# Reading the two parts of x in turns: 4, 16 or 64 columns at a time in a TensorE product

## The chip, the cores and the metric

The kernel runs on one core of one Trainium2 chip. The metric is device time in microseconds (us) of one execution, the median of several. The core's engines run side by side: TensorE (PE, with its weight loads as PEld), VectorE (DVE), ScalarE (ACT), GpSimd (POOL) and the queue that issues transfers (SP).

## What is computed

Two layers over 256 tokens of width 1024, all in float32. Layer 0 mixes tokens with a chunked gMLP, layer 1 with attention over 16 heads; after each mixer comes a gated MLP of width 2816 with a causal convolution of width 3. Each of the four sub-layers is `x <- LayerNorm(alpha * x + f(x))`. The lines of the reference that the change touches:

```python
def chunked_gmlp(x, w_in, ln_g, ln_b, w_s, b_s, w_out):
    z = jax.nn.gelu(x @ w_in)
    u, v = jnp.split(z, 2, axis=-1)
    ...
    return (u * sv.reshape(B, S, GMLP_WIDTH)) @ w_out

def moba_attention(x, w_qkv, w_o, rel_bias):
    qkv = (x @ w_qkv).reshape(B, S, 3, H, Dh)
    ...

def conv_ffn(x, w_up, conv_w, conv_b, w_down):
    h = x @ w_up
    ...
    return (jax.nn.gelu(g) * val) @ w_down
```

The products `x @ w_in` (its u half), `x @ w_qkv` (its query and key parts) and `x @ w_up` of layer 0 are the ones in question.

## The kernel before

**Two parts of each factor.** TensorE multiplies in float32r, a rounded form of float32. To keep float32 accuracy, each factor is split by `split` into a rounded part and the rest: weights into `whi` and `wlo`, activations into the high and low part that both lie in the tile `xt`. A product is then three products: high by high, high by low, and low by high.

**Where x lies.** `xt` holds, for each of the 8 blocks `k` of 128 input features, 512 columns: 256 tokens of the high part, and right behind them the same 256 tokens of the low part. `both[:, k]` is that run of 512 columns.

**Products by columns.** `cols_apart` (line 714) computes an output block of 128 features by 256 tokens. The weights stand in the array and x is streamed past them. In its first pass, for each of 8 `k`, one matmul with the weights `whi` streams all 512 columns of `both[:, k]`, and writes 512 columns of one accumulation bank: `whi` by x's high part into the first 256, `whi` by x's low part into the second 256. In its second pass, 8 matmuls with the weights `wlo` stream the 256 high columns alone and add to the second half. ACT then copies the second half out and DVE adds the first to it. `cols_apart` serves u in `gmlp` (stage `a_u`, 8 output blocks), queries and keys in `project` of `moba` (stage `b_qk`, 16 blocks), and 20 of the 22 block pairs of each up-projection in `conv_up` (stages `f_up0` and `f_up1`, 40 blocks each). The output bank is a tile called `bank`, or half of a tile called `twos`; in the up-projections the two kinds alternate.

**Order of the work.** All groups of instructions are recorded with an estimated cost and put in an order by `Plan.emit`; the cost of a matmul is taken from the number of its columns. `mms` (line 332) records a group, and line 344 in it issues every matmul of the stages in question. Each matmul comes with a weight load of its own, which the profile lists as PEld.

Of the kernel before, what the change touches and what calls it, by code (L numbers as in the profile page):

```python
# [35 lines left out]
HALF = 512  # L36
# [14 lines left out]
SOON = 5000.0  # L51
LEAD = 1700.0
WARM = 9


class Buf:
# [187 lines left out]
def trunk_kernel(ctx: ExitStack, tc: tile.TileContext, a: dict, out: bass.AP):  # L244
# [15 lines left out]
    both = xt.rearrange("p (k x) -> p k x", k=KT)  # L260
# [44 lines left out]
    def bank(long=False):  # L305
        free = [i for i in ALONE if not bank_of[i][2]]
        return taken(min(free, key=lambda i: bank_of[i][0]), long) if free else half(long)
# [18 lines left out]
    def done_with(b):  # L326
        for i in range(BANKS):
            if bank_of[i][1] is b:
                bank_of[i] = (bank_of[i][0], b, False)


    def mms(seq, r, w, fill=False, into=None, ready=False, share=1, turn=0.0):

        ns = 0.0
        for o, l, x, _, _ in seq:
            n = flat(x)
            ns += max(107.0, n / 2.4) + 2.5 if l.dtype == F32R else (218.0 if n <= P else n / 0.6 + 5)

        def emit():
            if into is not None and not ready:  # L340
                return

            for o, l, x, start, stop in seq if into is None else [q for _, _, q in sorted(into, key=lambda q: q[:2])]:
                nc.tensor.matmul(o, l, x, start=start, stop=stop)  # L344
        return plan.op("pe", ns / share + turn, emit, r, w, fill)
# [136 lines left out]
    def sub(name, c, s):  # L482
        return chunks[where[name, c]][s]

    def spent(name, c):
        i = where[name, c] + CHUNKS
        if i < len(stream):
            prep(i)
# [10 lines left out]
    def xt_new():  # L499
        return xth.new(), xtl.new()  # L500
# [4 lines left out]
    xh, xl = xt_new()  # L505
# [205 lines left out]
        plan.tick()  # L711
        return groups

    def cols_apart(*tiles):


        ops = []
        for low in (False, True):
            for b, at, h, l, hi, lo in tiles:
                o, wt = b.ap[:, at:at + HALF], lo if low else hi  # L720
                for k in range(KT):
                    ks, parts = slice(k * P, (k + 1) * P), [(t, k) for t in range(NT)]
                    seq = [(o[:, S:], wt.ap[:, ks], both[:, k, :S], False, k == KT - 1)] if low else \
                        [(o, wt.ap[:, ks], both[:, k], k == 0, False)]
                    ops.append(mms(seq, [(wt, [k // 2]), (h, parts)] + [(l, parts)] * (not low), [(b, [at])]))
                    plan.tick()
        return ops
# [76 lines left out]
    def xt_at(h, l):  # L804
        return lambda k, t: (xt_view(h)[:, t, k, :], xt_view(l)[:, t, k, :], [(h, [(t, k)]), (l, [(t, k)])])


    def gmlp():
        at = xt_at(xh, xl)
        pieces = [[(o, HALF, bank(True)) for o in (0, HALF)] for _ in range(NT)]  # L810
        order = [(k, t) for k in range(4) for t in range(NT)] + [(k, t) for t in range(NT) for k in range(4, KT)]
        v = []
        into, steps = [[] for _ in range(4)], {}
        for k, t in order:
            steps[k, t] = rows_step(pieces[t], *at(k, t), *sub("a_v", k // 2, k % 2), k == 0, k == KT - 1,
                                    into[k] if k < 4 else None)
            if (k, t) == (5, NT - 1):

                for j in (6, 7):
                    for o in steps[j, 0]:  # L820
                        o.after = steps[k, t][-1]
            if t == NT - 1 and k % 2:
                spent("a_v", k // 2)
            if (k, t) == (3, NT - 1):
                rows = ln_rows(0)
                ws, bs = load_mixer()
            if k == KT - 1:
                vt = place("ff", HALF + t * D, D)
                for o, n, b in pieces[t]:
                    act(vt.ap[:, o:o + n], b.ap, AF.Gelu_apprx_tanh, [b], [(vt, range(o // S, (o + n) // S))],  # L830
                        psum=True, table="gelu")
                    done_with(b)
                st, mean, rstd = stats(vt, vt.ap, [(0, HALF), (HALF, HALF)])
                scaled(vt, vt.ap, st, mean, rstd, rows)
                v.append(vt)
        load_rest()
        mh, ml = place("rr", 0, KT * S), place("rr", KT * S, KT * S)
        hv, lv = (b.ap.rearrange("p (k s) -> p k s", k=KT) for b in (mh, ml))
        uring = Places("ff", [0, S, HALF + 2 * D, HALF + 2 * D + S], S)
        yring = Places("ff", range(5120, 6144, S), S)  # L840
        uparts = Ring(tiles("uparts", 2, S))
        us = {}

        def spatial(gs):
            bs4 = [half() for _ in gs]
            o = mms([(b.ap[:, c * P:(c + 1) * P], v[c].ap[:, g * P:(g + 1) * P], ws[1][:, g, :], True, True)
                     for b, g in zip(bs4, gs) for c in range(NT)],
                    [(v[c], sorted({g // 2 for g in gs})) for c in range(NT)] + [ws[0]], bs4, fill=True)
            for b, g in zip(bs4, gs):
                y = yring.new()  # L850
                y3 = y.ap.rearrange("p (c t) -> p c t", c=NT)
                tt(y3, b.ap[:, :S].rearrange("p (c t) -> p c t", c=NT), bs[1][:, g:g + 1, :].to_broadcast([P, NT, P]),
                   ALU.add, [b, bs[0]], [y])
                if g < GROUPS // 2:
                    tt(y.ap, y.ap, us[g].ap, ALU.mult, [y, us[g]], [y])
                else:
                    plan.op("pool", 1060, lambda y=y, g=g: nc.gpsimd.tensor_tensor(y.ap, y.ap, us[g].ap, op=ALU.mult),
                            [y, us[g]], [y])
                split((mh, [g], hv[:, g, :]), (ml, [g], lv[:, g, :]), (y, [0], y.ap))
            return o  # L860

        for c in range(GROUPS // 2):
            pair = [bank(), bank()]
            ops = cols_apart(*((b, 0, xh, xl, *sub("a_u", c, j)) for j, b in enumerate(pair)))
            if c == 2:
                visit.after = ops[2 * KT - 1]
            spent("a_u", c)
            for g, b in zip((2 * c, 2 * c + 1), pair):
                us[g], part = uring.new(), uparts.new()
                for o in (act(part.ap, b.ap[:, S:], AF.Copy, [b], [part], psum=True),  # L870
                          tt(us[g].ap, b.ap[:, :S], part.ap, ALU.add, [b, part], [us[g]])):
                    o.early = SOON
                act(us[g].ap, us[g].ap, AF.Gelu_apprx_tanh, [us[g]], [us[g]], table="gelu")
            if c % 2:
                visit = spatial(range(2 * c - 2, 2 * c + 2))
        visit.after = ops[2 * KT - 1]
        return lambda k, t: (hv[:, k, t * P:(t + 1) * P], lv[:, k, t * P:(t + 1) * P], [(mh, [k]), (ml, [k])])


    def conv_up(layer, h, l):  # L880
# [6 lines left out]
        name = f"f_up{layer}"  # L887
# [45 lines left out]
        for t in range(NT):  # L933
            b = half()
# [13 lines left out]
        for n, i in enumerate(range(2, FT, 2)):  # L948
            subs = [sub(name, i + x, j) for x in range(2) for j in range(2)]
            if n % 2:  # L950
                bs = [two_banks(x) for x in range(2)]
                cols_apart(*((bs[m // 2], m % 2 * HALF, h, l, *s) for m, s in enumerate(subs)))
            else:
                bs = [bank() for _ in subs]
                cols_apart(*((b, 0, h, l, *s) for b, s in zip(bs, subs)))
            for x in range(2):
                spent(name, i + x)
                gate(i + x, joined(bs[x]) if n % 2 else joined_apart(bs[2 * x:2 * x + 2]), psum=False)
# [3 lines left out]
    def moba(h, l, scr):  # L962
# [28 lines left out]

        def project(i, visit=None):
            bs = [bank(), bank()]
            ops = cols_apart(*((bs[j], 0, h, l, *sub("b_qk", i, j)) for j in range(2)))
            if visit:
                visit(ops[2 * KT - 1])
            for j in range(2):
                part(i, j, bs[j])
            return ops[-1]
# [116 lines left out]
        n = PAIRS - 1  # L1116
# [20 lines left out]
    h, l = project_out("a_out", KT, at, xtok, 0, 1)  # L1137
    at = conv_up(0, h, l)
    scr = build_bias(10 * S)
    h, l = project_out("f_dn0", FT, at, xtok, 1, 2)  # L1140
    at = moba(h, l, scr)
    h, l = project_out("b_o", KT, at, xtok, 2, 3)
# [7 lines left out]
    ones = nc.const_aps.tensor(1.0, (P, HALF), mybir.dt.bfloat16)  # L1150
    for _ in range(WARM):
        nc.tensor.matmul(banks[-1], ones[:, :P], ones, start=True, stop=True)
# [82 lines left out]
```

## Time and profile before

| | |
|---|---|
| median of 3 runs | 561.52 us (561.39 to 561.65) |
| span of the profiled execution, first to last instruction | 560.6 us |
| PE busy | 553.1 us, 99% of the span, 3042 matmuls |
| PEld busy | 474.3 us, 85% |
| DVE busy | 470.9 us, 84% |
| ACT busy | 369.9 us, 66% |
| POOL busy | 15.0 us, 3% |
| HBM read | 109.36 MB, 197 GB/s over the span |

The profiled execution's span is 0.9 us under the median of the timed runs; that part lies around the first and last instruction. Matmuls overlap in the pipeline, so that the mean of one (391 ns for 512 columns) is the time from its start to its end, not the distance to the next. The rate of TensorE is read from starts: the difference between the starts of two pieces, divided by the matmuls of the first.

### The profile page before, as it was taken

The numbers are of one execution on the slowest core, as the hardware profiler recorded it, in microseconds if no ns is written. First come the engines' busy times: TensorE is split into PE (matmuls) and PEld (weight loads), VectorE is DVE, ScalarE is ACT, GpSimd is POOL, SyncE is SP. The second block draws the span as 40 slices with busy tenths as digits, with TensorE's granted clock in tenths as the row PEclk, the third lists the DMA queues.
The fourth block names the chain that finished last, engine by engine and source line by source line (L and its number), as shares of the span: only waits on it lengthen the run. The fifth ranks groups of instructions, "written<-read, shape, count | busy, mean of one in ns | idle before, by whom it ended". The sixth has DMA issues, their size and how long they took to land.

```text
span 560.6 us, 8337 instructions
## 1 busy us (share of the span) xinstructions
PE 553.1 (99%) x3042; PEld 474.3 (85%) x3042; DVE 470.9 (84%) x918; ACT 369.9 (66%) x700; POOL 15.0 (3%) x22
## 2 busy tenths in 40 slices
PE   9999999999999999999999999999999999999995
PEld 6889888988888888888888888788888988888884
DVE  5799989999998989467957788888999999998627
ACT  6657577786777767245567867578777787696601
POOL 0021110000000000001000000000000000000001
PEclk9999999999999999999999999999999999999999
DMA  8989414766555265752666351825757555467202
GB/s 321 374 317 329 175 75 161 290 233 229 214 188 189 80 248 214 260 220 76 229 221 198 104 189 76 300 77 176 275 205 275 196 188 189 166 215 292 79 0 77
DMA packets 19569, 110.98 MB, mean 198 GB/s; under 512 B 2294, under 2 KB 5576, under 8 KB 7368
## 3 DMA queue, kind: packets, MB, share of 16 engines
q1 hardware_dynamic: 19240, 110.18, 54.7%
q8 instruction: 24, 0.39, 0.3%
q10 hardware_dynamic: 288, 0.26, 0.1%
q14 instruction: 17, 0.14, 0.1%
HBM read 109.36 MB, written 1.07 MB: 197 GB/s over the span
## 4 chain that ended last, share of the span: by engine, by line
PE 96%; DVE 2%; DMA 1%; issue 0%; DVEq 0%; ACT 0%; ACTq 0%
PE bank L344 62%; PE twos L344 32%; PE twos L350 1%; PE bank L350 1%; DMA ff<-in_head 1%; DVE x L366 1%; DVE ff L366 0%; DVE stat L592 0%; DVE stat L632 0%; DVE whi L387 0%; DVE ff L635 0%; DVE x L362 0%; DVEq L1231 0%; DVE x L635 0%; DVE x L651 0%
## 5 line engine op out<-in xcount | busy, mean ns | idle before, releaser
L362 DVE TENSOR_TENSOR wlo<-raw,whi 128x1024 fp32r<-128x1024 f32 (+1 forms) x202 | 220.4, 1116 | 25.5 <-ACT whi L356 25.2
L356 ACT ACTIVATE whi<-raw 128x1024 fp32r<-128x1024 f32 (+1 forms) x202 | 187.4, 967 | 42.6 <-DMA raw<-in_f_dn 13.7
L344 PE MATMUL bank<-whi,rr 128*128 128x512 f32 x432 | 135.4, 391 | 0.0
L344 PE MATMUL bank<-xt,whi 128*128 128x512 f32 x512 | 121.2, 391 | 0.0
L344 PEld LDWEIGHTS bank<-xt,whi 128*128 128x128 f32 x512 | 94.7, 188 | 18.7
L344 PEld LDWEIGHTS bank<-whi,rr 128*128 128x128 f32 x432 | 81.1, 188 | 17.2 <-issue 0.5
L344 PE MATMUL bank<-wlo,rr 128*128 128x512 f32 x216 | 84.1, 389 | 0.0
L344 PE MATMUL twos<-xt,whi 128*128 128x512 f32 x320 | 74.4, 390 | 0.0
L366 DVE SCALAR_TENSOR_TENSOR ff<-ff,convc 128x255 f32<-128x255 f32 (+1 forms) x160 | 69.8, 479 | 2.9 <-ACT ff L356 2.6
L344 PEld LDWEIGHTS twos<-xt,whi 128*128 128x128 f32 x320 | 59.4, 188 | 11.9
L344 PEld LDWEIGHTS bank<-xt,wlo 128*128 128x128 f32 x512 | 64.2, 191 | 2.0 <-issue 0.3
L344 PE MATMUL bank<-xt,wlo 128*128 128x256 f32 x512 | 65.6, 284 | 0.0
L356 ACT ACTIVATE ff<-ff,convc 128x256 f32<-128x256 f32 x80 | 45.6, 593 | 10.8 <-DVE ff L362 10.7
L344 PEld LDWEIGHTS bank<-wlo,rr 128*128 128x128 f32 x216 | 40.6, 188 | 8.1
L344 PE MATMUL twos<-whi,xt 128*128 128x512 f32 x128 | 42.1, 396 | 0.0
L344 PEld LDWEIGHTS twos<-xt,wlo 128*128 128x128 f32 x320 | 39.7, 192 | 0.8
L344 PE MATMUL twos<-xt,wlo 128*128 128x256 f32 x320 | 40.0, 283 | 0.0
L356 ACT ACTIVATE ff<-ff 128x256 f32<-128x256 f32 x52 | 20.4, 412 | 26.8 <-DVE rr L362 20.5
L356 ACT ACTIVATE ff<-bank 128x256 f32<-128x256 f32 (+2 forms) x62 | 24.2, 395 | 17.5 <-PE bank L344 16.2
L356 ACT ACTIVATE ff<-bank,lncol 128x128 f32<-128x128 f32 x48 | 18.9, 459 | 22.1 <-PE bank L350 18.5
L356 ACT ACTIVATE ff<-twos 128x512 f32<-128x512 f32 (+1 forms) x34 | 17.7, 551 | 16.1 <-PE twos L344 13.4
L344 PEld LDWEIGHTS twos<-whi,xt 128*128 128x128 f32 x128 | 24.1, 188 | 4.8
(113 smaller groups left out, 530.1 us busy)
## 6 DMA issues: line engine op xcount, KB each, us to landing
raw<-in_f_up SPq DMA_DIRECT2D x44, 1024.0 KB, 4.8
raw<-in_f_dn SPq DMA_DIRECT2D x22, 1024.0 KB, 4.8
raw<-in_b_qk SPq DMA_DIRECT2D x8, 1024.0 KB, 4.8
lnrow<-in_lnrow SPq DMA_DIRECT2D x5, 1024.0 KB, 6.7
raw<-in_a_out SPq DMA_DIRECT2D x4, 1024.0 KB, 7.3
raw<-in_b_v SPq DMA_DIRECT2D x4, 1024.0 KB, 4.8
raw<-in_b_o SPq DMA_DIRECT2D x4, 1024.0 KB, 4.9
raw<-in_a_u SPq DMA_DIRECT2D x3, 1024.0 KB, 9.7
```

The costliest lines, as they stand in the source:

```text
L344: nc.tensor.matmul(o, l, x, start=start, stop=stop)
L350: nc.tensor.transpose(o, x, ident.ap)
L356: return plan.op("act", ns, lambda: nc.scalar.activation(o, x, func, **kw), r, w, table=table)
L362: return dve(70 + 1.04 * flat(x), lambda: nc.vector.tensor_tensor(o, x, y, op=op), r, w)
L366: lambda: nc.vector.scalar_tensor_tensor(o, x, s, y, op0=op0, op1=op1), r, w)
```

## The change

A table `TURNS` gives three stages a number of columns, and the first pass of `cols_apart` takes the same 512 columns of x in another order: `n` columns of the high part, `n` of the low part, the next `n` of the high part, and so on. The output pattern is rearranged in the same way, so that each result lands where it landed before. The second pass, `f_up1` and all other products stay as they were.

```diff
+TURNS = {"a_u": 4, "b_qk": 16, "f_up0": 64}
...
-    def cols_apart(*tiles):
+    def in_turns(ap, n):
+
+        return ap.rearrange("p (a g e) -> p g a e", a=2, e=n) if n else ap
+
+    def cols_apart(*tiles, turns=0):
...
-                        [(o, wt.ap[:, ks], both[:, k], k == 0, False)]
+                        [(in_turns(o, turns), wt.ap[:, ks], in_turns(both[:, k], turns), k == 0, False)]
...
-            ops = cols_apart(*((b, 0, xh, xl, *sub("a_u", c, j)) for j, b in enumerate(pair)))
+            ops = cols_apart(*((b, 0, xh, xl, *sub("a_u", c, j)) for j, b in enumerate(pair)), turns=TURNS["a_u"])
...
-                cols_apart(*((bs[m // 2], m % 2 * HALF, h, l, *s) for m, s in enumerate(subs)))
+                cols_apart(*((bs[m // 2], m % 2 * HALF, h, l, *s) for m, s in enumerate(subs)), turns=TURNS.get(name, 0))
...
-                cols_apart(*((b, 0, h, l, *s) for b, s in zip(bs, subs)))
+                cols_apart(*((b, 0, h, l, *s) for b, s in zip(bs, subs)), turns=TURNS.get(name, 0))
...
-            ops = cols_apart(*((bs[j], 0, h, l, *sub("b_qk", i, j)) for j in range(2)))
+            ops = cols_apart(*((bs[j], 0, h, l, *sub("b_qk", i, j)) for j in range(2)), turns=TURNS["b_qk"])
```

In the built program no instruction moves: all five engines have the same instructions in the same order with the same waits. What differs is the pattern of 512 matmuls on PE. At the start of u, PE's rows before are the following (output tile, moving and standing operand, output shape, how many in a row; lines of the changed kernel are numbered one higher):

```order
L344 MATMUL bank_110<-whi_72,xt 128x512
L344 MATMUL bank_107<-xt,whi_73 128x512 x8
L344 MATMUL bank_108<-xt,whi_74 128x512 x8
L344 MATMUL bank_107<-xt,wlo_83 128x256 x8
L344 MATMUL bank_108<-xt,wlo_84 128x256 x8
```

The same place after:

```order
L345 MATMUL bank_110<-whi_72,xt 128x512
L345 MATMUL bank_107<-xt,whi_73 128x64x2x4 x8
L345 MATMUL bank_108<-xt,whi_74 128x64x2x4 x8
L345 MATMUL bank_107<-xt,wlo_83 128x256 x8
L345 MATMUL bank_108<-xt,wlo_84 128x256 x8
```

Each high pass is still 8 matmuls per output block, now of 64 turns by 2 parts by 4 columns; the low pass is untouched.

At the start of the first up-projection's products by columns, where two small groups of transposes stand between them, PE has before:

```order
L344 MATMUL bank_109<-xt,whi_73 128x512 x8
L344 MATMUL bank_110<-xt,whi_74 128x512
L350 MATMUL twos_105<-ident,ff 128x128 x2
L350 MATMUL twos_106<-ident,ff 128x128 x2
L344 MATMUL bank_110<-xt,whi_74 128x512 x7
```

And after:

```order
L345 MATMUL bank_109<-xt,whi_73 128x4x2x64 x8
L345 MATMUL bank_110<-xt,whi_74 128x4x2x64
L351 MATMUL twos_105<-ident,ff 128x128 x2
L351 MATMUL twos_106<-ident,ff 128x128 x2
L345 MATMUL bank_110<-xt,whi_74 128x4x2x64 x7
```

The transposes stay at the same matmul; the shape now is 4 turns by 2 parts by 64 columns. In queries and keys it is 16 turns by 2 parts by 16 columns, in the same way.

## The prediction

> **What bounds the kernel now.** I read the page's head first, then the chain that ended last, then what PE waited for, and then PE's timeline in each stage that uses products by columns.
>
> ```profile
> span 560.6 us, 8337 instructions
> PE 553.1 (99%) x3042; PEld 474.3 (85%) x3042; DVE 470.9 (84%) x918; ACT 369.9 (66%) x700; POOL 15.0 (3%) x22
> PEclk9999999999999999999999999999999999999999
> PE 96%; DVE 2%; DMA 1%; issue 0%; DVEq 0%; ACT 0%; ACTq 0%
> ```
>
> PE works 99% of the span at the full granted clock, and 96% of the chain that ended last is PE. So a change of PE's rate goes into the time one to one, unless another engine takes over. The waits of PE over the whole execution, with total, count and longest in us, are two:
>
> ```profile
> PE twos L1152 <- PEq L1228: 0.8, 1, 0.8
> PE bank L344 <- DVE whi L387: 0.4, 1, 0.4
> ```
>
> Both lie at the very start (the warm-up and the first weights). In the changed stages PE waits for nobody, and there is no stall that could go away. What is left is the rate of the matmuls themselves. PE's timeline gives it: start, duration of the piece, line, tiles, count. Here are u, then the first up-projection, then queries and keys, then the second up-projection, which the change leaves alone:
>
> ```profile
> 27.78 3.79 PE L344 MATMUL bank<-xt,whi 128*128 128x512 f32 x16
> 31.40 2.08 PE L344 MATMUL bank<-xt,wlo 128*128 128x256 f32 x16
> 33.31 3.82 PE L344 MATMUL bank<-xt,whi 128*128 128x512 f32 x16
> ...
> 100.52 7.44 PE L344 MATMUL twos<-xt,whi 128*128 128x512 f32 x32
> 107.80 4.00 PE L344 MATMUL twos<-xt,wlo 128*128 128x256 f32 x32
> 111.63 7.44 PE L344 MATMUL bank<-xt,whi 128*128 128x512 f32 x32
> ...
> 284.44 3.79 PE L344 MATMUL bank<-xt,whi 128*128 128x512 f32 x16
> 288.07 2.08 PE L344 MATMUL bank<-xt,wlo 128*128 128x256 f32 x16
> ...
> 394.06 7.44 PE L344 MATMUL twos<-xt,whi 128*128 128x512 f32 x32
> 401.34 4.00 PE L344 MATMUL twos<-xt,wlo 128*128 128x256 f32 x32
> ```
>
> From start to start a matmul of 512 columns takes (31.40 - 27.78) / 16 = 226 ns in u, (107.80 - 100.52) / 32 = 227.5 ns in the first up-projection, (288.07 - 284.44) / 16 = 227 ns in queries and keys, and (401.34 - 394.06) / 32 = 227.5 ns in the second up-projection. A matmul of 256 columns takes (111.63 - 107.80) / 32 = 119.7 ns. The difference of 107.8 ns over 256 columns is 0.42 ns per column; 227.5 - 512 x 0.42 leaves a fixed 12 ns per matmul. The rate is the same in all stages, whatever else goes on: the two windows of u have a DMA share of 0.47 and 0.96 and both are filled by PE.
>
> ```profile
> 27.78:31.40 3.62, 3.62 (x17) 1.00 0.47 149
> 31.40:33.31 1.91, 1.91 (x17) 1.00 0.96 386
> ```
>
> So a product by columns costs columns times 0.42 ns plus 12 ns, and nothing that the profile shows disturbs it.
>
> **The change part by part.** How many matmuls change follows from the code and two groups of the page, which together hold all first passes of products by columns:
>
> ```profile
> L344 PE MATMUL bank<-xt,whi 128*128 128x512 f32 x512 | 121.2, 391 | 0.0
> L344 PE MATMUL twos<-xt,whi 128*128 128x512 f32 x320 | 74.4, 390 | 0.0
> ```
>
> The two rows are 832 = 8 k times (8 blocks of u + 16 of queries and keys + 40 + 40 of the two up-projections). The change takes 64 in u, 128 in queries and keys and 320 in the first up-projection: 512 of the 832.
>
> 1. Instructions, their order and their waits: the same on every engine, as the built program shows; each changed matmul is still one instruction with one weight load. Cost 0, and there is no queue past which anything moves.
>
> 2. Columns: 512 per matmul as before, and 512 x 0.42 + 12 = 227 ns if a column costs the same wherever it lies. Cost 0.
>
> 3. Jumps. Before, the 512 columns are one run. After, u has 2 x 64 = 128 runs per matmul, queries and keys 32, the first up-projection 8. New jumps: 64 x 127 + 128 x 31 + 320 x 7 = 8128 + 3968 + 2240 = 14336. At each jump the read address in `xt` and the write address in the bank step by about 256 columns, back or forth. No matmul of the trace has more than one run, so this price is not shown and has to be bounded.
>
> The nearest rows are instructions of ACT and DVE with several runs, beside rows of the same size with one run. `xt<-ff` writes 512 elements of `xt` in runs of 128, so three jumps; `ff<-twos` reads two runs of 256 out of an accumulation tile, one jump; `whi<-ff`, `ff<-bank` and `wlo<-ff,whi` have one run (mean ns in the last number before the idle time):
>
> ```profile
> L356 ACT ACTIVATE xt<-ff 128x512 fp32r<-128x512 f32 x8 | 5.0, 632 | 0.1
> L356 ACT ACTIVATE whi<-ff 128x512 fp32r<-128x512 f32 x7 | 4.3, 626 | 1.6 <-DMA ff<-in_head 1.5
> L356 ACT ACTIVATE ff<-twos 128x512 f32<-128x512 f32 x20 | 11.8, 592 | 13.4 <-PE twos L344 13.4
> L356 ACT ACTIVATE ff<-bank 128x512 f32<-128x512 f32 x4 | 2.3, 594 | 3.2 <-PE bank L344 3.1
> L362 DVE TENSOR_TENSOR xt<-ff,xt 128x512 fp32r<-128x512 f32 x8 | 5.4, 689 | 0.6 <-ACT xt L356 0.4
> L362 DVE TENSOR_TENSOR wlo<-ff,whi 128x512 fp32r<-128x512 f32 x8 | 5.3, 688 | 0.9 <-ACT whi L356 0.8
> ```
>
> Per jump that is (632 - 626) / 3 = 2 ns, 592 - 594 = -2 ns, and (689 - 688) / 3 = 0.3 ns. They lie on both sides of zero, and one such instruction varies by more than that: 684 to 693 ns in the group of `wlo<-ff,whi`.
>
> ```profile
> L362 DVE TENSOR_TENSOR wlo<-ff,whi x8: 684/686/693, 5.5 to 11.8; 128x512 fp32r<-128x512 f32 x8
> ```
>
> So the rows show no price of a jump that stands out of their noise; the upper end is 2 ns, or 14336 x 2 = 28.7 us. A jump can hardly gain time, since the 512 columns go by one after the other. The lower end is that the fixed 12 ns went away with the new order: 512 x 12 = 6.1 us less. I take 0, because the row that is nearest in kind (DVE, reading and writing `xt` itself) differs by 1 ns in 689.
>
> 4. What hides a cost here: nothing. PE has no idle time in these stages, so each ns of PE counts. What follows on others: the results of a bank come free at the same matmul as before, and ACT and DVE read them in the same pattern as before.
>
> [...]
>
> Sum: 560.6 us of span + 0 + 0.9 us around it = 561.5 us, the median of the runs shown.
>
> **The rivals.**
>
> - A jump costs about one column. Then 14336 x 0.42 = 6.0 us, 567.5 us; u pays 8128 x 0.42 = 3.4 of it, queries and keys 1.7, the up-projection 0.9. For it speaks that a column takes only 0.42 ns, against 626 / 512 = 1.2 ns per element on ACT and 688 / 512 = 1.3 on DVE, so that those rows could hide one column's delay; against it, that they show no sign of a price. At 0.08 ns per jump it is still within what can be told (1.1 us).
>
> - Runs of 4 columns are too short to keep the stream full, runs of 16 are long enough. Then u alone pays: at half the rate, 64 x 512 x 0.42 = 13.8 us, 575.3 us. For it speaks that the shortest run of the rows above is 128 elements, so that nothing here shows a run of 4; against it, that no window shows it disturbed by a DMA share of 0.96. The point that decides is whether u's 226 ns stay.
>
> - The broken pattern itself slows the matmul, however long its runs are: at half the rate in all three stages, 512 x 512 x 0.42 = 110 us, 671 us. The timeline holds no row for it or against it. [...]
>
> - The other sign: the fixed 12 ns is a wait at the start of each matmul that depends on the order of addresses, and the turns shorten it. All of it gone would be 561.5 - 6.1 = 555.4 us. For it speaks that 12 ns is not explained by columns; against it, that it is the same with 512 and 256 columns and in stages with other traffic. DVE would not stop this gain: it is busy 104.09 of 112 us in the first up-projection, where the gain would be 320 x 12 ns = 3.8 us.
>
> ```profile
> 89.00:201.00 112.00, 112.00 (x647) 99.16 (x646) 104.09 (x190) 82.50 (x149) 0.00 (x0) 1.00 0.57 204
> ```
>
> - That the change doesn't do what it says (a matmul cut into several, each with a weight load of its own) is excluded by the built program: one instruction per matmul.
>
> **How the numbers follow.** A difference of 0.2%, 1.1 us, is about what a measurement of this kernel can tell from no change. Chances: no change 0.59 (561.5 us, 560.4 to 562.6); a price per jump 0.18 (567.5 us, from 562.6 up to 590 at 2 ns); u alone at half rate 0.07 (575.3 us); the pattern itself 0.06 (671 us); a gain 0.10 (555.4 to 560.4 us). Slower is 0.18 + 0.07 + 0.06 = 0.31. The range must leave out no more than 2 in 10: from 560.4 to 575.4 us it holds no change (0.59), u at half rate (0.07) and some two thirds of the price per jump (up to 1 ns each, 0.13), together 0.79. It leaves out the gain, the high prices and the pattern.
>
> **What would show it.** In the changed kernel's timeline each piece of 16 or 32 first-pass matmuls should keep its 226 to 227.5 ns per start, in u, in queries and keys and in the first up-projection, and the second up-projection is the measure that nothing else moved. A price per jump shows as 127 : 31 : 7 in the extra time of one matmul in u, in queries and keys and in the up-projection; short runs show in u alone; a price of the pattern shows equally in all three. A gain shows as starts closer than 226 ns. I am wrong if any of the three stages leaves that rate by more than some 2 ns per matmul (512 x 2 = 1.0 us), or if PE shows idle time for DVE or ACT in them.

## The result, and the profile after

The change makes the kernel slower: 564.62 us median (564.33 to 566.42) against 561.52 us, ratio 1.006 with a 95% interval of 1.0048 to 1.0072. The extra is 3.1 us. (The ratios of this document are taken over all runs, so they need not be those of the two medians.)

The head of the page of the changed kernel:

```profile
span 562.6 us, 8337 instructions
PE 555.2 (99%) x3042; PEld 474.1 (84%) x3042; DVE 471.0 (84%) x918; ACT 370.3 (66%) x700; POOL 14.3 (3%) x22
PEclk9999999999999999999999999999999999999999
```

PE is busy 2.1 us longer, the other engines as before, and the granted clock is 0.999 of full, as before. PE's waits are again only those of the very start:

```profile
PE twos L1157 <- PEq L1233: 0.8, 1, 0.8
PE bank L345 <- DVE whi L388: 0.3, 1, 0.3
```

So no wait came in; the matmuls themselves take longer. PE's timeline at the three changed stages (start, duration of the piece, tiles, count), in the order u, first up-projection, queries and keys:

```profile
27.08 4.17 PE L345 MATMUL bank<-xt,whi 128*128 128x512 f32 x16
31.09 2.07 PE L345 MATMUL bank<-xt,wlo 128*128 128x256 f32 x16
...
101.13 7.44 PE L345 MATMUL twos<-xt,whi 128*128 128x512 f32 x32
108.41 4.00 PE L345 MATMUL twos<-xt,wlo 128*128 128x256 f32 x32
...
285.03 4.00 PE L345 MATMUL bank<-xt,whi 128*128 128x512 f32 x16
288.87 2.07 PE L345 MATMUL bank<-xt,wlo 128*128 128x256 f32 x16
```

From start to start a changed matmul takes (31.09 - 27.08) / 16 = 250.6 ns in u, where it was 226 to 229, 228 on the mean of u's four pieces. In queries and keys it takes (288.87 - 285.03) / 16 = 240 ns where it was 227 to 229. In the first up-projection it takes (108.41 - 101.13) / 32 = 227.5 ns, as before. These are, in this order, runs of 4, 16 and 64 columns. The extras are 64 x (250.6 - 228) = 1.4 us for u and 128 x (240 - 228) = 1.5 us for queries and keys, 3.0 us in all, against the 3.1 us that were measured. The two profiled spans differ by 2.0 us only, because u began at 27.08 us here and at 27.78 us in the profile of before; from u's start on, the difference is (562.6 - 27.08) - (560.6 - 27.78) = 2.7 us.

### The profile page after: what moved, and what is told of

Same layout as the page of the kernel before. It is cut to its first block, busy times and chain, and to the rows that moved or that the text cites. A ratio compares the mean times of both kernels' runs of the same rounds, so it can differ in the third digit from the quotient of the medians.

```text
span 562.6 us, 8337 instructions
## 1 busy us (share of the span) xinstructions
PE 555.2 (99%) x3042; PEld 474.1 (84%) x3042; DVE 471.0 (84%) x918; ACT 370.3 (66%) x700; POOL 14.3 (3%) x22
## 4 chain that ended last, share of the span: by engine, by line
PE 96%; DVE 2%; DMA 1%; issue 0%; DVEq 0%; ACT 0%; ACTq 0%
PE bank L345 62%; PE twos L345 32%; PE twos L351 1%; PE bank L351 1%; DMA ff<-in_head 1%; DVE x L367 1%; DVE ff L367 0%; DVE stat L593 0%; DVE stat L633 0%; DVE whi L388 0%; DVE ff L636 0%; DVE x L363 0%; DVEq L1236 0%; DVE x L636 0%; DVE x L652 0%
## 5 line engine op out<-in xcount | busy, mean ns | idle before, releaser
L345 PE MATMUL bank<-xt,whi 128*128 128x512 f32 x512 | 124.2, 397 | 0.0
L345 PEld LDWEIGHTS twos<-xt,whi 128*128 128x128 f32 x320 | 59.4, 188 | 11.9
L357 ACT ACTIVATE ff<-ff,convc 128x256 f32<-128x256 f32 x80 | 45.6, 593 | 10.7 <-DVE ff L363 10.6
L345 PEld LDWEIGHTS twos<-xt,wlo 128*128 128x128 f32 x320 | 39.7, 192 | 0.8
```

The source lines that it names most:

```text
L357: return plan.op("act", ns, lambda: nc.scalar.activation(o, x, func, **kw), r, w, table=table)
```

## The experiments

**1. Each stage alone.** Two kernels keep the turns in one stage.

```diff
-TURNS = {"a_u": 4, "b_qk": 16, "f_up0": 64}
+TURNS = {"a_u": 4, "b_qk": 0, "f_up0": 0}
```

```diff
-TURNS = {"a_u": 4, "b_qk": 16, "f_up0": 64}
+TURNS = {"a_u": 0, "b_qk": 16, "f_up0": 0}
```

> Only u reads in turns (4 columns). Theory that each stage adds its own matmuls' extra: 64 x (250.6 - 228.0) = +1.4 us over before, ratio 1.0026, and the queries and keys at 227 ns again. Rival (the first stage's extra vanishes in the transfers that u waits for, or moves the start of what follows): ratio within 0.9995 to 1.0010.

> Only queries and keys read in turns (16 columns). Theory that each stage adds its own matmuls' extra: 128 x (240.1 - 228.0) = +1.5 us over before, ratio 1.0028. Rival (u carries all 3.1 us, and queries and keys hide theirs behind the softmax): ratio within 0.9995 to 1.0010.

Measured: u alone 563.05 us against 561.53, ratio 1.0026 (1.0016 to 1.0035); queries and keys alone 562.84 us, ratio 1.0022 (1.0013 to 1.0031). Both rivals fall: each stage carries its own extra, and together they make the whole (1.0048 against 1.006; the two intervals leave room for it).

**2. All lengths of run in one kernel.** Each step of the up-projections gets its own length, with 32 first-pass matmuls each, so one trace holds the whole series next to steps that read straight.

```diff
-TURNS = {"a_u": 4, "b_qk": 16, "f_up0": 64}
+TURNS = {"a_u": 0, "b_qk": 0, "f_up0": (0, 128, 64, 32, 16, 8, 4, 2, 0, 0), "f_up1": (0, 2, 4, 8, 16, 32, 64, 128, 0, 0)}
...
-                cols_apart(*((bs[m // 2], m % 2 * HALF, h, l, *s) for m, s in enumerate(subs)), turns=TURNS.get(name, 0))
+                cols_apart(*((bs[m // 2], m % 2 * HALF, h, l, *s) for m, s in enumerate(subs)), turns=TURNS[name][n])
...
-                cols_apart(*((b, 0, h, l, *s) for b, s in zip(bs, subs)), turns=TURNS.get(name, 0))
+                cols_apart(*((b, 0, h, l, *s) for b, s in zip(bs, subs)), turns=TURNS[name][n])
```

> u and queries and keys read x straight again; in each up-projection the blocks of one loop step share a length of run: none, 128, 64, 32, 16, 8, 4, 2, none, none in the first, none, 2, 4, 8, 16, 32, 64, 128, none, none in the second. Start to start of a first-pass matmul of 512 columns, beside 227 ns. Theory 1 (a fixed price per jump, sized by u's 24 ns for 127 jumps, 0.19 ns): 128 +0.6, 64 +1, 32 +3, 16 +6, 8 +12, 4 +24, 2 +48. Theory 2 (one column, 0.42 ns, per jump, sized by queries and keys): 64 +3, 32 +6, 16 +13, 8 +26, 4 +53, 2 +107. Theory 3 (the stage matters, not the length of run: the up-projection's matmuls have slack that the others lack): all lengths from 4 up stay near 227. Theory 4 (a price that starts under a certain length of run and then levels off): 64 +0, 16 +13, 4 +24 as in the three stages of the changed kernel, with 32 and 8 between their neighbours.

PE's timeline of this kernel, first up-projection, from the step with 64 columns to the step with 2 columns:

```profile
111.11 7.44 PE L345 MATMUL bank<-xt,whi 128*128 128x512 f32 x32
118.39 4.00 PE L345 MATMUL bank<-xt,wlo 128*128 128x256 f32 x32
122.22 7.73 PE L345 MATMUL twos<-xt,whi 128*128 128x512 f32 x32
129.79 4.00 PE L345 MATMUL twos<-xt,wlo 128*128 128x256 f32 x32
133.62 7.84 PE L345 MATMUL bank<-xt,whi 128*128 128x512 f32 x32
141.30 3.99 PE L345 MATMUL bank<-xt,wlo 128*128 128x256 f32 x32
145.13 7.95 PE L345 MATMUL twos<-xt,whi 128*128 128x512 f32 x32
152.91 3.99 PE L345 MATMUL twos<-xt,wlo 128*128 128x256 f32 x32
156.74 8.17 PE L345 MATMUL bank<-xt,whi 128*128 128x512 f32 x32
164.75 4.00 PE L345 MATMUL bank<-xt,wlo 128*128 128x256 f32 x32
168.59 10.83 PE L345 MATMUL twos<-xt,whi 128*128 128x512 f32 x32
179.24 4.02 PE L345 MATMUL twos<-xt,wlo 128*128 128x256 f32 x32
```

| run, columns | 64 | 32 | 16 | 8 | 4 | 2 |
|---|---|---|---|---|---|---|
| ns per matmul | 227.5 | 236.6 | 240 | 243 | 250.3 | 333 |
| over 227.5 | 0 | 9 | 12.5 | 16 | 23 | 105 |

Each number is the difference of two starts by 32; 128 columns give 227.8 (107.28 - 99.99, the step before these). The second up-projection takes the lengths in reverse order; that its extras are about the same is an estimate from the whole time below. The values of 16 and 4 are those of the changed stages, so the stage does not matter (theory 3 falls). Neither does a fixed price per jump hold. Theory 1 meets 4 columns, by which it was sized, but it asked for 48 at 2 columns and for 3 at 32, where 105 and 9 were measured. Theory 2 meets 16, by which it was sized, and also 2 columns (107 against 105), but between them it asked for 26 at 8 and 53 at 4, where 16 and 23 were measured. Theory 4 is right in that 64 is free and that 32 and 8 lie between their neighbours; it is wrong in that the price levels off, since 2 columns cost 105 ns. The time, 572.36 us in one run, is 10.8 us above before; 2 x 32 x (9 + 12.5 + 16 + 23 + 105) ns is 10.6 us.

**3. Reading and writing apart.** The pattern of `xt` and that of the bank are now chosen separately for each step; "near" takes the even runs first and then the odd ones, "far" the turns of the change. A shifted read starts `how[2]` columns later; the last of the 8 blocks, which has no block behind it, then reads the first block once more.

```diff
+FORMS = {"far": "p (a g e) -> p g a e", "near": "p (g a e) -> p a g e"}
...
+        at = k % (KT - 1) * 2 * S + how[2]
+        return xt[:, at:at + 2 * S]
...
-                        [(in_turns(o, turns), wt.ap[:, ks], in_turns(both[:, k], turns), k == 0, False)]
+                        [(in_turns(o, turns[1]), wt.ap[:, ks], in_turns(part_of(k, turns[0]), turns[0]), k == 0, False)]
```

> The reading of x and the writing to the bank are broken up separately, in the steps of the two up-projections (results of the blocks concerned land in other places than they should; the work is the same in amount). First: straight, read 16, write 16, both 16, read 4, write 4, both 4, read 4 shifted by 2 columns, both 16 near, straight. Second: straight, both 4 near, read 16 shifted by 2 columns, read 8, write 8, both 8, both 64 near, read 16 near, write 16 near, straight. Near means that first the even and then the odd runs are taken, so that a jump goes over one run, not over 256 columns. Extra per matmul beside 227 ns. Theory R (the reading of xt is what costs): read 16 +13, read 4 +24, write 16 and write 4 +0. Theory W (the writing to the bank costs): the reverse, write 16 +13, write 4 +24, read +0. Theory B (half from each): about 6 and 12 each. If the distance of the jump matters, near 16 and near 4 cost less than 13 and 24; if only the breaks matter, the same. [...]

PE's timeline, in this order: read 16, write 16, read 4, write 4, read 4 shifted by 2 columns, both 4 near, read 16 shifted by 2 columns.

```profile
99.94 7.84 PE L351 MATMUL twos<-xt,whi 128*128 128x512 f32 x32
107.62 3.99 PE L351 MATMUL twos<-xt,wlo 128*128 128x256 f32 x32
111.44 7.44 PE L351 MATMUL bank<-xt,whi 128*128 128x512 f32 x32
118.72 4.00 PE L351 MATMUL bank<-xt,wlo 128*128 128x256 f32 x32
...
134.06 8.17 PE L351 MATMUL bank<-xt,whi 128*128 128x512 f32 x32
142.07 4.00 PE L351 MATMUL bank<-xt,wlo 128*128 128x256 f32 x32
145.91 7.44 PE L351 MATMUL twos<-xt,whi 128*128 128x512 f32 x32
153.19 4.00 PE L351 MATMUL twos<-xt,wlo 128*128 128x256 f32 x32
...
168.87 11.04 PE L351 MATMUL twos<-xt,whi 128*128 128x512 f32 x32
179.74 4.00 PE L351 MATMUL twos<-xt,wlo 128*128 128x256 f32 x32
...
399.66 7.63 PE L351 MATMUL twos<-xt,whi 128*128 128x512 f32 x32
407.13 3.99 PE L351 MATMUL twos<-xt,wlo 128*128 128x256 f32 x32
410.96 9.55 PE L351 MATMUL bank<-xt,whi 128*128 128x512 f32 x32
420.34 4.01 PE L351 MATMUL bank<-xt,wlo 128*128 128x256 f32 x32
```

Reading in turns of 16 alone takes 240 ns and of 4 alone 250.3 ns: the whole extra. Writing in turns of 16 or 4 alone takes 227.5 ns: nothing. Theory R holds, W and B fall. The distance of the jump matters for short runs only: 4 near takes 233.4 ns (+6 instead of +23), while 16 near takes 239.7 ns, as far 16 does, and 64 near is free like 64 far. Shifting the runs of 4 by 2 columns takes 339.7 ns, 89 more than runs of 4 in their place and about what runs of 2 cost; runs of 16 shifted by 2 take 293 ns, which is 53 more. The time, 571.59 us in one run, is 10.1 us above before; the extras of the steps by 32 matmuls each add up to 9.9 us.

**4. Places of runs, and the shorter second pass.**

```diff
+FORMS = {"far": "p (a g e) -> p g a e", "near": "p (g a e) -> p a g e"}
...
+rd, wr, low = (lambda *x: (x, None, None)), (lambda *x: (None, x, None)), (lambda *x: (None, None, x))
...
+         "f_up0": (NO, rd("all", 0, 2), wr("far", 2), wr("near", 2), low("far", 32), low("far", 16), low("far", 64),
+                   rd("near", 32), rd("far", 64, 2), NO),
+         "f_up1": (NO, rd("near", 8), low("far", 8), low("far", 4), rd("all", 0, 4), rd("far", 4, 4),
+                   rd("far", 16, 4), rd("far", 16, 8), rd("far", 32, 16), NO)}
...
-                    seq = [(o[:, S:], wt.ap[:, ks], both[:, k, :S], False, k == KT - 1)] if low else \
-                        [(in_turns(o, turns), wt.ap[:, ks], in_turns(both[:, k], turns), k == 0, False)]
+                    seq = [(o[:, S:], wt.ap[:, ks], in_turns(both[:, k, :S], turns[2]), False, k == KT - 1)] if low else \
+                        [(in_turns(o, turns[1]), wt.ap[:, ks], in_turns(part_of(k, turns[0]), turns[0]), k == 0, False)]
```

In the second pass (`low`) the turns are taken between the two halves of its 256 columns, so that a far jump goes over 128 columns there.

> More places and lengths of runs in the steps of the two up-projections (results of the blocks concerned land in other places than they should; the work is the same in amount). First: straight, read straight but shifted by 2 columns, write 2, write 2 near, low pass (256 columns) read in turns of 32, of 16, of 64, read near 32, read 64 shifted by 2 columns, straight. Second: straight, read near 8, low pass read 8, low pass read 4, read straight but shifted by 4 columns, read 4 shifted by 4, read 16 shifted by 4, read 16 shifted by 8, read 32 shifted by 16, straight. Theory J (what counts is the number of jumps in a matmul): the low pass with 32 has 8 runs and costs nothing over its 119.7 ns, with 16 it has 16 runs and costs +9, with 8 +13, with 4 +16. Theory N (what counts is the length of a run, and the price is a share of the columns): low 64 +0, low 32 +4.5, low 16 +6, low 8 +8, low 4 +11. [...] Writes in runs of 2: +0 if the accumulation bank takes pairs, about +100 if it is like the reading.

PE's timeline, in this order: read straight shifted by 2 columns, write 2, read 64 shifted by 2; then the second pass read in turns of 8 and of 4, and the first pass read straight shifted by 4, read 4 shifted by 4 and read 16 shifted by 4.

```profile
100.01 7.63 PE L352 MATMUL twos<-xt,whi 128*128 128x512 f32 x32
107.47 4.00 PE L352 MATMUL twos<-xt,wlo 128*128 128x256 f32 x32
111.31 7.44 PE L352 MATMUL bank<-xt,whi 128*128 128x512 f32 x32
118.59 4.00 PE L352 MATMUL bank<-xt,wlo 128*128 128x256 f32 x32
...
178.24 8.27 PE L352 MATMUL bank<-xt,whi 128*128 128x512 f32 x32
186.34 3.88 PE L352 MATMUL bank<-xt,wlo 128*128 128x256 f32 x31
...
413.34 4.11 PE L352 MATMUL bank<-xt,wlo 128*128 128x256 f32 x32
417.28 7.43 PE L352 MATMUL twos<-xt,whi 128*128 128x512 f32 x32
424.55 4.22 PE L352 MATMUL twos<-xt,wlo 128*128 128x256 f32 x32
428.60 7.57 PE L352 MATMUL bank<-xt,whi 128*128 128x512 f32 x32
436.01 4.00 PE L352 MATMUL bank<-xt,wlo 128*128 128x256 f32 x32
439.85 8.18 PE L352 MATMUL twos<-xt,whi 128*128 128x512 f32 x32
447.86 3.99 PE L352 MATMUL twos<-xt,wlo 128*128 128x256 f32 x32
451.68 7.84 PE L352 MATMUL bank<-xt,whi 128*128 128x512 f32 x32
459.36 3.99 PE L352 MATMUL bank<-xt,wlo 128*128 128x256 f32 x32
```

Writing in pairs is still free (227.5 ns, far and near). Shifts by a multiple of 4 columns change nothing on the broken reads that were tried: runs of 4 shifted by 4 take 250.3 ns, runs of 16 take 240 ns shifted by 4 and 240.3 shifted by 8, and runs of 32 shifted by 16 take 236.6, each within 0.3 ns of its unshifted time. A shift by 2 does cost: runs of 64 take 253.1 ns, 26 more than unshifted. A straight read takes 233.1 ns shifted by 2 columns (6 more) and 231.6 shifted by 4 (4 more). Nor does a shift by 2 have a fixed price per run: with experiment 3, it adds 89, 53 and 26 ns for 128, 32 and 8 runs, which is 0.7, 1.7 and 3.2 ns per run. Reading near, 8 takes 232.5 ns (5 more, where far it was 16) and 32 takes 236.6, as far 32 does. The second pass of 256 columns takes 123.1 ns in turns of 8 and 126.6 ns in turns of 4, 3.4 and 6.9 over 119.7; in turns of 64, 32 and 16 it is within 1 ns of 119.7. Both J (13 and 16) and N (8 and 11) expected more, so the step of 9 ns that the first pass takes between 64 and 32 columns is missing in the second pass. The time was 565.42 us in one run, 3.8 us above before, which is the sum of the extras of its steps by 32 matmuls each (3.7 us).

**5. The change's two halves, timed.** One kernel keeps the read order, the other the write order.

```diff
-                        [(in_turns(o, turns), wt.ap[:, ks], in_turns(both[:, k], turns), k == 0, False)]
+                        [(o, wt.ap[:, ks], in_turns(both[:, k], turns), k == 0, False)]
```

> The change with its read order alone (4, 16, 64 as in the change); the bank is written straight, so that the results of these blocks land in other places than they should. Theory R (the reading carries the whole loss): ratio to before as with the whole change, 1.005 to 1.006, u at 250 ns, queries and keys at 240 ns, up-projection at 227.5 ns. Theory W (the writing carries it): 1.000.

```diff
-                        [(in_turns(o, turns), wt.ap[:, ks], in_turns(both[:, k], turns), k == 0, False)]
+                        [(in_turns(o, turns), wt.ap[:, ks], both[:, k], k == 0, False)]
```

> The change with its write order alone; x is read straight, so that the results of these blocks land in other places than they should. Theory R: ratio to before 0.999 to 1.001, all three stages at 227 ns. Theory W: 1.005 to 1.006.

Measured: reading alone 564.95 us against 561.63, ratio 1.0052 (1.0039 to 1.0064); writing alone 561.59 us, ratio 0.9998 (0.9989 to 1.0007). The loss is in the reading of `xt`.

**6. 64 columns everywhere.**

```diff
-TURNS = {"a_u": 4, "b_qk": 16, "f_up0": 64}
+TURNS = {"a_u": 64, "b_qk": 64, "f_up0": 64}
```

> 64 columns in all three stages. Theory that runs of 64 columns are free wherever they stand: ratio to before 0.999 to 1.001, all stages at 227 ns. Rival (u and the queries and keys are sensitive as stages, the up-projection is not): 1.002 to 1.006.

Measured: 561.64 us against 561.63, ratio 0.9999 (0.9990 to 1.0008), with the first piece of u at 226.9 ns per matmul and that of queries and keys at 226.3; the up-projection, at 64 columns in the change too, kept its 227.5 ns there. None of the kernels here is faster than the kernel before beyond the noise.

**7. The lengths dealt out anew,** to see whether the table of experiment 2 foretells a time.

```diff
-TURNS = {"a_u": 4, "b_qk": 16, "f_up0": 64}
+TURNS = {"a_u": 16, "b_qk": 4, "f_up0": 32}
```

> The change with its lengths dealt out anew: 16 columns in u, 4 in queries and keys, 32 in the first up-projection. Theory that the length of run alone sets a matmul's extra, whichever stage it stands in, and that it goes into the time one to one: 64 x 12 + 128 x 22 + 320 x 9 = 0.8 + 2.8 + 2.9 = 6.5 us over before, ratio 1.0115, with matmuls at 240, 250 and 236.5 ns in the three stages. Rival (a part of it is hidden, or the up-projection's is, whose extra no timed run has shown yet): 1.006 or less.

Measured: 568.08 us against 561.98, ratio 1.0111 (1.0094 to 1.0128); expected 1.0115. Its timeline, u, then a step of the first up-projection, then queries and keys:

```profile
26.85 4.00 PE L345 MATMUL bank<-xt,whi 128*128 128x512 f32 x16
30.69 2.07 PE L345 MATMUL bank<-xt,wlo 128*128 128x256 f32 x16
...
111.89 7.73 PE L345 MATMUL bank<-xt,whi 128*128 128x512 f32 x32
119.46 3.99 PE L345 MATMUL bank<-xt,wlo 128*128 128x256 f32 x32
...
287.00 4.17 PE L345 MATMUL bank<-xt,whi 128*128 128x512 f32 x16
291.01 2.07 PE L345 MATMUL bank<-xt,wlo 128*128 128x256 f32 x16
```

That is 240 ns at 16 columns, 236.6 at 32 and 250.6 at 4: the length of run sets the extra, in whichever stage it stands, and, within the interval of the time, all of it reaches the end.

## Why the prediction was wrong, and where it was right

It forecast no change, and the kernel is 0.6% slower.

**Right: what bounds the kernel.** PE has no idle time in these stages, so every ns of a matmul goes into the time. Experiments 1 and 7 show the sum of the matmuls' extras as the time, to 0.2 us in the first pair and 0.4 us in the last. Step 1 holds as well: the same instructions and waits, and no new wait of PE. So does step 2's number of columns; its condition, that a column costs the same wherever it lies, is what the runs refute.

**Wrong: step 3, the price of a jump.** It took 0 for all 14336 jumps, and that is true for the 2240 of the first up-projection only. The others cost 23 ns per matmul in u and 12 to 12.5 in queries and keys, 1.4 and 1.5 us. This is also the prediction's own sign of being wrong: two of the three stages left their rate by more than 2 ns per matmul. The value came from rows of ACT and DVE whose shortest run was 128 elements. Those rows agree with what PE does: runs of 128 and 64 are free there too (227.8 and 227.5 ns). They said nothing of runs of 4 and 16, nor of TensorE (what such runs cost ACT and DVE was not measured either), and the text saw that ("nothing here shows a run of 4") in a rival and did not let it weigh on the sum. The step also priced reading and writing together; the runs show that one side costs all and the other nothing. That 564.62 us lies in the stated range is no merit of the sum: above 562.6 us the range was there for the rivals.

**The rivals.** The price per jump came nearest: a slowdown of the matmuls in place, without a wait, though with 6.0 us it was twice what was measured. Its size of one column per jump (0.42 ns) fits queries and keys, 12.5 / 31 = 0.40 ns, but not u, 23 / 127 = 0.18 ns, nor the up-projection, 0. Its ratio of 127 : 31 : 7 is not what stands in the trace. The rival that runs of 4 are too short had the right sense of a length, but u is at 250 ns and not at half the rate, and runs of 16 cost too (240 ns). The broken pattern as such costs nothing: 64 columns everywhere have ratio 0.9999, and writes in runs of 16, 8, 4 and 2 columns keep 227.5 ns. No run shows the half rate of its 671 us (some 455 ns per matmul); the slowest matmuls of 512 columns, runs of 4 shifted by 2, took 339.7. The gain did not come: no changed stage is under its rate of before.

**Open.** Why runs of 64 are free and runs of 32 cost 9 ns at once in a matmul of 512 columns, and nothing in one of 256, is not settled. Neither the number of jumps nor the length of run alone gives it: 16 runs of 32 cost 9 ns, 16 runs of 16 in the second pass cost 0.3 ns. The two passes do differ by nearly a constant: for 15, 31 and 63 far jumps the first pass pays 9, 12.5 and 16 ns and the second 0.3, 3.4 and 6.9, some 9 ns less each time. So from 15 to 63 jumps the price grows alike in both, and what is open is the step of 9 ns. That the second pass jumps over 128 columns and not over 256 does not explain it, as near 32 costs the same 9 ns as far 32. Weight loads, which run beside the reading, leave hardly a gap in the second pass: in the page of the kernel before, those of `twos<-xt,wlo` are idle 0.8 us beside 39.7 us busy, those of `twos<-xt,whi` in the first pass 11.9 beside 59.4. Whether an extra of the reading hides behind them was not tried.

## What to carry to other kernels

A row that prices a pattern counts only for runs as long as its own; where the new pattern is far shorter than any in the trace, the price is open, and it has to be split into reading and writing. In a kernel that TensorE bounds, keep what a float32r matmul of 512 columns streams past the weights in unshifted runs of 64 columns or more: these took 227.5 to 227.8 ns, against 236.6 in runs of 32 and 253.1 in runs of 64 shifted by 2 columns. In these experiments the results could be scattered over the accumulation bank in turns of 16, 8, 4 or 2 columns at no cost (227.5 ns). When a rate is in question, give each step of a loop another value: one trace then holds the whole series.

## What the runs showed of the hardware

- A float32r matmul of 512 columns whose moving operand is read in turns from places 256 columns apart takes 227.5 ns from start to start with runs of 64 columns, 227.8 with 128, 236.6 with 32, 240 with 16, 243 with 8, 250 with 4 and 333 with 2. Writing the results in runs of 16, 8, 4 or 2 keeps 227.5 ns.
- A read shifted by 2 columns took 89 ns more with runs of 4 (339.7 ns), 53 more with runs of 16 (293) and 26 more with runs of 64 (253.1), while a shift by 4 added nothing to runs of 4 and 16, one by 8 nothing to runs of 16 and one by 16 nothing to runs of 32. A straight read of 512 columns took 227.5 ns in its place, 231.6 shifted by 4 columns and 233.1 shifted by 2.
- Jumps over one run of 4 columns cost 6 ns per matmul, jumps over 256 columns with the same runs 23; with runs of 8 it is 5 and 16, with runs of 16 (240 ns) and 32 (236.6) the distance makes no difference.
- A float32r matmul of 256 columns takes 119.7 ns, 123.1 read in turns of 8 and 126.6 in turns of 4; turns of 64, 32 and 16 change it by less than 1 ns.
